# Two attentions that normalise their probabilities early and turn half-precision planes by DMA; gate factors written as rows

## The chip, the core and the metric

The kernel runs on one core of one Trainium2 chip. A core has a matrix engine (TensorE, PE in the profile; its weight loads are listed apart as PEld), a vector engine (VectorE, DVE), a scalar engine (ScalarE, ACT), GpSimd (POOL) and SyncE (SP), which mostly issues DMAs. Each engine runs its own instructions in order; semaphores tie the engines together. Matrix products read from the on-chip memory SBUF and write to PSUM. The metric is device time in microseconds (us) of one execution; times are compared by the median of several runs.

## The reference

The computation is two layers of a diffusion backbone with 512 latent tokens and 256 context tokens, model width 1024. Each layer normalises and modulates its input, makes one combined projection, and runs two attention branches side by side. Branch A is a 2-D neighbourhood attention (8 heads of 64; latent queries see a window of 8 rows by 16 columns, with a learned position bias, and all context keys). Branch B is grouped-query attention (8 query heads, 2 key heads, all latent and context keys, rotary positions). The softmax of both is the usual one:

```
s = einsum(q, k).astype(float32) * HEAD_DIM ** -0.5      (+ bias in branch A)
p = softmax(s, axis=-1).astype(v.dtype)
att = einsum(p, v)
o_a = (a_att * silu(a_z)) @ w_o_a
o_b = (b_att * silu(b_z)) @ w_o_b
merged = sigmoid(g_a) * o_a + sigmoid(g_b) * o_b
x_new = x + gate_x * (merged @ w_out)
```

The first layer also updates the context tokens, which attend to context only; the second layer leaves them. `gate_x` (and `gate_c` for the context) is one third of `silu(c) @ w_ada + b_ada`. All inputs and the output are float32.

## The kernel before, in words

Products keep float32 accuracy by splitting: a value is written as a rounded high part and a low remainder, and each product of two split operands is three matrix products (lines 429 to 431, `mm3`). Weights are loaded as raw tiles by SP, cast to a high part on ACT and subtracted on DVE or GpSimd (`load_w`, `load_w2`; tiles raw, whi, wlo).

The layer runs as: projections of branch A's keys, values and queries; NA, head by head; projections of branch B; GQ, head by head; then the output projections ("merge"). `pipeline` runs the heads: it issues the scores of head h, then the value products of head h-1, then some pieces of `fill`, independent projections (the gates and SiLU paths) that give PE work between the attention's steps. The order on each engine is made by a scheduler from this program order; buffers are rotating pools, and a tile is written again only when its readers are done.

In NA (`na_scores`, `na_values`) a head has four query tiles of 128, one of them the edge tile of the grid. For each tile PE makes 512 scores in PSUM (pss), DVE adds the bias and finds the greatest (L954, tile p), ACT takes the exponential with its sum (L957), and `softmax_tail` divides: DVE takes the reciprocal r of the sum and multiplies p by it and by one half, or, for query tiles 1 and 3 (`NA_POOL`), GpSimd does the multiplying (L763, L764). One head later, `transpose_split` turns p: PE transposes 128x128 blocks against an identity (L773, L775), ACT copies the result from PSUM as the high part (L781), DVE subtracts it for the low part (L782). There are four such groups of four transposes per head, and one more for the context queries in layer 0. The value products (L977 to L988) take both parts, with values split in va0 and va1.

In GQ (`gq_scores`, `gq_values`) a tile has 768 scores. DVE's pass L1127 finds the greatest value and shifts it by a constant (`P_LOG`), ACT takes the exponential (L1128), and `turned` makes two float16 planes of the undivided p: a cast on ACT (L798) and a subtraction on DVE, or on GpSimd for tiles 1 and 3 (L799), into a tile h. SP then issues a transposing DMA from h to ht (L800). The value products (L1144, L1145) read ht. The division comes last: `divide` turns the reciprocals by PE (L807) and multiplies them into the gate path (L808). `head_out` adds the two halves of the product and multiplies by the gate path z (L791 to L793). The context queries of layer 0 go the same way (tiles ct), with the subtraction on GpSimd.

The bias of NA is loaded by SP for each head (`load_bias`, L929 and L931) into single buffers. Issued by SP as well: the weight loads, the reloads of spilled gates (L656), and the gate factors. `ada_gate` makes the factors as a tile [128, 8 per vector] and writes them to DRAM transposed, element by element (L317); the merge stage reads them back as a row.

Of the kernel before, what the change touches and what calls it, by code (L numbers as in the profile page):

```python
# [25 lines left out]
NP_NA = (7, 8)  # L26
# [3 lines left out]
NT_NA = 2  # L30
P_LOG = 9.7
# [39 lines left out]
def hybrid_kernel(es: ExitStack, tc, x, ctx, cvec, w_ada, w_ada0, small, gvec, w_in, w_o_a, w_o_b, w_out,  # L71
# [238 lines left out]
    def ada_gate(l, nv):  # L310
# [6 lines left out]
        nc.sync.dma_start(gd[l][0:n].rearrange("n p -> p n"), g[:, 0:nv].rearrange("p v k -> p (v k)"))  # L317
# [232 lines left out]
    def split_v(ps, hi, lo, hi_src=None):  # L550
        S.copy(R(hi), ps)
        V.tensor_tensor(R(lo), ps, hi, ALU.subtract)

    def evac_va(dsts):
        def f(t, ps):
            d = dsts[t // 3].rearrange("p (t n) -> p t n", t=3)[:, t % 3, :]
            d = d.rearrange("p (r q d) -> p r q d", q=4, d=64)
            s = ps.rearrange("p (r e d) -> p r e d", e=2, d=64)
            hi, lo = d[:, :, 0:4:3, :], d[:, :, 1:3, :]
            split_v(s, hi, lo)  # L560
        return f
# [18 lines left out]
    def layer(l, hx, nxt, start):  # L580
# [8 lines left out]
        def gate_steps(halves, pool):  # L589
            return (ada_steps(l, range(16, 24), halves, nv, pool)  # L590
                    + ([lambda: ada_gate(l, nv)] if 1 in halves else []))
# [133 lines left out]
        va = [big("va0"), big("va1")]  # L725
        w = load_w(W, C_AV, 512, KT, mix_lo)
        for t in range(6):
            tok_proj(w, 512, a_hx, t, evac_va(va))
# [16 lines left out]
        for t in range(qt):  # L745
            tok_proj(w, 512, a_hx, t, evac_na(qav, True, gq, YB if first else 4))
            run(bg, per_bg)
# [7 lines left out]
        if True:  # L755
            def softmax_tail(p, n, r, pieces, eng=None):

                V.reciprocal(r, r)
                for i, (c0, c1) in enumerate(pieces):
                    if eng is None:  # L760
                        V.tensor_scalar(p[:, c0:c1], p[:, c0:c1], r[:, i:i + 1], 0.5, ALU.mult, ALU.mult)
                    else:
                        G.tensor_scalar(r[:, i:i + 1], r[:, i:i + 1], 0.5, None, ALU.mult)  # L763
                        G.tensor_tensor(p[:, c0:c1], p[:, c0:c1],  # L764
                                        r[:, i:i + 1].to_broadcast([128, c1 - c0]), ALU.mult)

            def transpose_split(blocks, n0=0, n1=512):

                att["turn"] += 1
                pt = psw(512, "s" if att["spare"] and att["turn"] % 2 else "t")  # L770
                for src, c0 in blocks:
                    if c0 is None:
                        T.transpose(pt.rearrange("p (s n) -> p s n", n=64)[:, 0:8:7, :], src, ident)  # L773
                    else:
                        T.transpose(pt[:, c0:c0 + 128], src, ident)  # L775
                if att["spare"]:
                    hi, lo = R(p_tile()[:, 0:512]), R(p_tile()[:, 0:512])
                else:
                    hi = att["p"].tile([128, 512], F32R, tag="pth", name=nm("pth"), bufs=att["nt"])
                    lo = att["p"].tile([128, 512], F32R, tag="ptl", name=nm("ptl"), bufs=att["nt"])  # L780
                S.copy(hi[:, n0:n1], pt[:, n0:n1])  # L781
                V.tensor_tensor(lo[:, n0:n1], pt[:, n0:n1], F(hi[:, n0:n1]), ALU.subtract)  # L782
                return hi, lo

            def head_out(po, e, dst, eng=None):
# [5 lines left out]
                S.copy(a, po[o:o + 64, :n])  # L791
                V.tensor_tensor(a, po[m:m + 64, :n], a, ALU.add)
                (eng or G).tensor_tensor(dst, dst, a, ALU.mult)  # L793

            def turned(p, n, out, eng):

                h = att["p"].tile([128, 2, n], F16, tag="h", name=nm("h"), bufs=att["nh"])
                S.copy(h[:, 0], p[:, :n])  # L798
                eng.tensor_tensor(h[:, 1], p[:, :n], h[:, 0], ALU.subtract)  # L799
                nc.sync.dma_start_transpose(out, h.rearrange("p a n -> p (a n)"))  # L800

            def divide(ps, r, e, dst, back):

                n = r.shape[-1]
                V.reciprocal(r, r)
                for i in range(n):
                    T.transpose(ps[:, 128 * i:128 * i + 128], r[:, i:i + 1].to_broadcast([128, 128]), ident)  # L807
                V.scalar_tensor_tensor(dst, ps[64 * e:64 * e + 64, :128 * n], back[64 * e:64 * e + 64], dst,  # L808
                                       ALU.mult, ALU.mult)

            def shrink(v, s, mx, row):

                V.tensor_reduce(mx[:, 0:1], v, AX, ALU.max)
                V.tensor_reduce(mx[:, 1:2], v, AX, ALU.min, negate=True)
                V.tensor_tensor(mx[:, 0:1], mx[:, 0:1], mx[:, 1:2], ALU.max)
                pt = psw(512, "t")
                T.transpose(pt[0:1, 0:128], mx[:, 0:1], ident)
                V.tensor_reduce(row[:, 0:1], pt[0:1, 0:128], AX, ALU.max)
                T.matmul(pt[:, 128:129], row[:, 0:1].to_broadcast([1, 128]), ident[0:1, 0:1], start=True, stop=True)
                V.tensor_scalar(s[:, 1:2], pt[:, 128:129], 1.0e-30, 1.0 / V_UP, ALU.max, ALU.mult)  # L820
                V.reciprocal(s[:, 0:1], s[:, 1:2])
                V.tensor_scalar(s[:, 1:2], s[:, 1:2], 0.5, None, ALU.mult)
# [40 lines left out]
            def ctx_scores(q, kh, kl, ct=None):  # L863
# [7 lines left out]
                if ct is not None:  # L871
                    V.tensor_scalar(mx, mx, P_LOG, None, ALU.add)
                p = p_tile()
                r = sp.tile([128, 2], F32, tag="r", name=nm("r"), bufs=8)
# [3 lines left out]
                if ct is not None:  # L878
                    turned(p, 512, ct.rearrange("p a i k n -> p (a i k) n"), G)
                    return ct, r  # L880
                softmax_tail(p, 512, r, [(0, 256), (256, 512)])
                return p

            def ctx_values(p, vsl, dst, e, back=None):
                if back is not None:
                    ct, r = p
                    ps = psw(512, "v")
                    po = ps[:, 0:256]
                    divide(ps[:, 256:512], r, e, dst, back)
                    for k in range(2):  # L890
                        for a in range(2):
                            T.matmul(po.rearrange("p (i n) -> p i n", i=2), vsl(4 + k), ct[:, a, :, k, :],
# [603 lines left out]
```

## Time and profile before

| | us |
|---|---|
| median of three runs | 1131.86 |
| lowest, highest | 1130.71, 1135.87 |
| profiled execution | 1136.54 |
| its span in the trace | 1134.8 |
| busy PE, DVE, ACT, POOL | 1092.4, 765.3, 578.0, 490.5 |

The profile is of one execution. Busy time is the union of an engine's instructions; matrix products overlap each other, so a busy PE need not be at its peak rate. A line of the groups gives source line, engine, operation, tiles, shapes and count, then busy time and the mean ns of one, then the idle time just ahead of it with what ended it. "SPq" and the like are the queues in which an engine issues DMAs. A row of the waits gives the waiting engine and line, what it waited for, then total us, number of times, and the longest.

### The profile page before, as it was taken

To read this page: it belongs to the slowest core of one execution; us is meant where nothing else is said; L and a number is where in the kernel's file an instruction comes from. 1 tells how busy PE (TensorE), PEld (TensorE's weight loads), DVE (VectorE), ACT (ScalarE), POOL (GpSimd) and SP (SyncE) were. 2 spreads that over 40 slices of the span, in tenths; PEclk is the share of its full clock that TensorE was granted. 3 is DMA by queue.
4 is the path that set the end of the run, shared out by engine and by line. 5 is a ranking of instruction groups with operands and counts; after the bars stand their busy time and mean duration, and the time that the engine had idled before them with its cause. 6 is when DMAs were issued, how large, how long until landed. Compare 5 with 4: busy or idle time off the path is not lost.

```text
span 1134.8 us, 16867 instructions
## 1 busy us (share of the span) xinstructions
PE 1092.4 (96%) x5824; PEld 905.5 (80%) x5824; DVE 765.3 (67%) x1492; ACT 578.0 (51%) x1152; POOL 490.5 (43%) x405
## 2 busy tenths in 40 slices
PE   8999999999999999779999999999999999999998
PEld 5688888888988877557788888887888987777677
DVE  4666788888365478636567895357988765677473
ACT  6463266656333566555331275325666545776431
POOL 1044255654246245345521454335554563463530
PEclk9999999999999999989999999999999999999999
DMA  9454412233341597679733542453333236989742
GB/s 366 148 173 134 126 49 66 83 125 98 110 140 47 130 205 176 108 216 248 192 104 127 158 149 77 142 182 72 108 105 112 64 103 164 186 219 250 198 147 81
DMA packets 195278, 161.29 MB, mean 142 GB/s; under 512 B 119444, under 2 KB 161144, under 8 KB 193528
## 3 DMA queue, kind: packets, MB, share of 16 engines
q1 hardware_dynamic: 187856, 145.82, 47.2%
q0 software_dynamic: 2368, 7.87, 2.1%
q10 hardware_dynamic: 4968, 6.53, 1.7%
q8 instruction: 46, 0.75, 0.3%
q14 instruction: 40, 0.33, 0.1%
HBM read 115.58 MB, written 17.32 MB: 117 GB/s over the span
## 4 chain that ended last, share of the span: by engine, by line
PE 78%; DMA 6%; DVE 5%; issue 5%; POOL 3%; ACT 2%; SPq 1%; POOLq 0%; ACTq 0%; DVEq 0%
PE psx L431 11%; PE psx L430 11%; PE psx L429 11%; PE psf L429 9%; PE psf L430 8%; PE psf L431 8%; PE pst L775 2%; PE pss L951 2%; PE pss L857 2%; PE pss L858 2%; DMA raw<-in_w_in_dram 2%; DMA ht<-h 1%; PE pst L521 1%; PE pst L1144 1%; PE pst L1145 1%
## 5 line engine op out<-in xcount | busy, mean ns | idle before, releaser
L429 PE MATMUL psf<-hx,whi 128*128 128x512 f32 (+1 forms) x360 | 137.9, 383 | 4.1 <-ACT zt L610 2.5
L416 POOL TENSOR_TENSOR wlo<-raw,whi 128x512 fp32r<-128x512 f32 x70 | 98.0, 1405 | 94.4 <-ACT whi L414 64.3
L431 PE MATMUL psf<-hx,wlo 128*128 128x512 f32 (+1 forms) x360 | 135.8, 377 | 0.0
L430 PE MATMUL psf<-hx,whi 128*128 128x512 f32 (+1 forms) x360 | 135.2, 376 | 0.0
L429 PE MATMUL psx<-whi,hx 128*128 128x512 f32 (+1 forms) x328 | 120.7, 371 | 0.0
L430 PE MATMUL psx<-wlo,hx 128*128 128x512 f32 (+1 forms) x328 | 119.7, 366 | 0.0
L431 PE MATMUL psx<-whi,hx 128*128 128x512 f32 (+1 forms) x328 | 119.5, 365 | 0.0
L414 ACT CAST whi<-raw 128x512 fp32r<-128x512 f32 x136 | 82.5, 620 | 72.6 <-DMA raw<-in_w_in_dram 44.9
L402 POOL TENSOR_TENSOR wlo<-raw,whi 128x512 fp32r<-128x512 f32 x40 | 61.0, 1528 | 120.6 <-ACT whi L399 73.0
L799 POOL TENSOR_TENSOR h<-p,h 128x768 f16<-128x768 f32 (+1 forms) x40 | 64.9, 1626 | 99.7 <-ACT h L798 79.1
L399 ACT CAST whi<-raw 128x512 fp32r<-128x512 f32 x88 | 54.4, 623 | 100.4 <-PE psx L431 33.9
L500 POOL TENSOR_TENSOR ss<-ss,ehalf 128x8 f32<-128x8 f32 (+2 forms) x40 | 62.2, 1558 | 74.1 <-DVE ss L497 74.0
L416 DVE TENSOR_TENSOR wlo<-raw,whi 128x512 fp32r<-128x512 f32 x66 | 66.6, 1009 | 28.9 <-ACT whi L414 27.4
L1127 DVE CUSTOM_DVE_ANT_0 p<-pss,vb 128x768 f32<-128x768 f32 x64 | 60.2, 953 | 36.7 <-PE pss L858 19.9
L429 PEld LDWEIGHTS psf<-hx,whi 128*128 128x128 f32 x360 | 67.9, 189 | 16.1 <-ACT zt L610 3.6
L431 PEld LDWEIGHTS psf<-hx,wlo 128*128 128x128 f32 x360 | 67.8, 188 | 11.5
L430 PEld LDWEIGHTS psf<-hx,whi 128*128 128x128 f32 x360 | 67.9, 189 | 10.3
L1128 ACT ACTIVATE p<-pss,mx 128x768 f32<-128x768 f32 x64 | 57.5, 900 | 35.0 <-DVE mx L1127 31.5
L431 PEld LDWEIGHTS psx<-whi,hx 128*128 128x128 f32 x328 | 61.9, 189 | 10.0
L430 PEld LDWEIGHTS psx<-wlo,hx 128*128 128x128 f32 x328 | 62.0, 189 | 9.2
L429 PEld LDWEIGHTS psx<-whi,hx 128*128 128x128 f32 x328 | 61.7, 189 | 8.9
L429 PE MATMUL psx<-hx,whi 128*128 128x256 f32 (+1 forms) x208 | 68.1, 327 | 0.0
(359 smaller groups left out, 3097.5 us busy)
## 6 DMA issues: line engine op xcount, KB each, us to landing
raw<-in_w_in_dram SPq DMA_DIRECT2D x168, 256.0 KB, 2.9
rawb<-in_w_ada_dram SPq DMA_DIRECT2D x48, 256.0 KB, 2.8
raw<-in_w_out_dram SPq DMA_DIRECT2D x32, 256.0 KB, 3.1
tg<-gs SPq DMA_DIRECT2D x4, 1536.0 KB, 6.4
rawx<-in_w_ada_dram SPq DMA_DIRECT2D x4, 1024.0 KB, 13.3
rawy<-in_w_ada_dram SPq DMA_DIRECT2D x4, 1024.0 KB, 10.3
gs<-zt ACTq DMA_DIRECT2D x16, 256.0 KB, 2.1
raw<-in_w_o_a_dram SPq DMA_DIRECT2D x16, 256.0 KB, 3.4
```

Of the source, the lines that this page charges most:

```text
L399: S.copy(hi[:, :n], raw[:, :n])
L402: e.tensor_tensor(lo[:, :n], raw[:, :n], F(hi[:, :n]), ALU.subtract)
L414: S.copy(hi, raw)
L416: lo_eng(i).tensor_tensor(lo, raw, F(hi), ALU.subtract)
L429: T.matmul(ps, lhs[0], rhs[0], start=first, stop=False)
L430: T.matmul(ps, lhs[0], rhs[1], start=False, stop=False)
L431: T.matmul(ps, lhs[1], rhs[0], start=False, stop=last)
L500: G.tensor_tensor(ss, ss, ehalf[:, :n], ALU.pow)
L775: T.transpose(pt[:, c0:c0 + 128], src, ident)
L799: eng.tensor_tensor(h[:, 1], p[:, :n], h[:, 0], ALU.subtract)
L1127: V.tensor_tensor_reduce(p, pss, lift, -1.0, 3e38, ALU.add, ALU.min, mx[:, 0:1])
L1128: S.activation(p, pss, AF.Exp, bias=mx[:, 0:1], accum_out=r[:, i:i + 1])
```

## The change

Both attentions now divide before they turn. `turned` replaces `softmax_tail`, `transpose_split` and `divide`. It takes the reciprocal of the row sums, scales it by 2 to the 14th (`P_UP`), and makes two float16 planes of the normalised p. On query tiles 0 and 2, ACT's cast applies the factor and DVE does multiply and subtract in one instruction; on tiles 1 and 3 GpSimd scales r, multiplies p, and subtracts, with ACT's plain cast in between. Context tiles take the first form, two halves each. SP then issues the transposing DMAs; NA's edge tile needs two of them, for 64 rows each, as its columns of the turned tile lie apart.

NA's values become float16 planes too: each of the six tiles is copied to vf and its greatest magnitude found by an absolute-value pass on ACT and a maximum on DVE (`size`); after the first query tile `split_va` makes one common factor (`shrink`, two small PE steps) and the planes (`halves`). Two of the nine large buffers change their use: vf and one f16 tile in place of va0 and va1, and then `spare` for the turned tiles of even heads and the context. `head_out` applies the factor back. The pools are smaller: p tiles 3 and 4 by layer in place of 7 and 8, h tiles 3 and 4. NA's products no longer use the PSUM pool v for latent queries.

In GQ, DVE's shift by a constant gives way to a plain maximum. The factors of `ada_gate` are turned by PE, copied by ACT and written as whole rows.

```diff
+        pt = psw(512, "t")
+        T.transpose(pt[0:n, 0:128], g[:, 0:nv].rearrange("p v k -> p (v k)"), ident)
+        gt = pool.tile([16, 128], F32, tag="agt", name=nm("agt"), bufs=1)
+        S.copy(gt[0:n], pt[0:n, 0:128])
+        nc.sync.dma_start(gd[l][0:n], gt[0:n])
-        nc.sync.dma_start(gd[l][0:n].rearrange("n p -> p n"), g[:, 0:nv].rearrange("p v k -> p (v k)"))
...
+    def size(v, junk, mx):
+        S.activation(junk, v, AF.Abs)
+        V.tensor_reduce(mx, junk, AX, ALU.max)
+    def halves(v, d, s):
+        S.activation(d[:, :, 0, :], v, AF.Copy, scale=s)
+        V.scalar_tensor_tensor(d[:, :, 1, :], v, s, d[:, :, 0, :], ALU.mult, ALU.subtract)
...
+            def turned(p, n, out, eng, r=None):
+                h = att["p"].tile([128, 2, n], F16, tag="h", name=nm("h"), bufs=att["nh"])
+                if r is not None:
+                    V.reciprocal(r, r)
+                    eng.tensor_scalar(r, r, P_UP, None, ALU.mult)
+                    w = n // r.shape[-1]
+                if r is None or eng is G:
+                    if r is not None:
+                        G.tensor_tensor(p, p, r.to_broadcast([128, n]), ALU.mult)
+                    S.copy(h[:, 0], p[:, :n])
+                    eng.tensor_tensor(h[:, 1], p[:, :n], h[:, 0], ALU.subtract)
+                else:
+                    for i in range(n // w):
+                        c = slice(w * i, w * i + w)
+                        S.activation(h[:, 0, c], p[:, c], AF.Copy, scale=r[:, i:i + 1])
+                        V.scalar_tensor_tensor(h[:, 1, c], p[:, c], r[:, i:i + 1], h[:, 0, c], ALU.mult, ALU.subtract)
+                for o, (n0, n1) in out:
+                    nc.sync.dma_start_transpose(o, h[n0:n1].rearrange("p a n -> p (a n)"))
...
             def na_scores(h, q, kh, kl):
-                    softmax_tail(p, 512, r[:, 0:1], [(0, 512)], G if i in NA_POOL else None)
+                    at = [(0, 64, 0), (448, 512, 64)] if i == 0 else [(128 * i - 64, 128 * i + 64, 0)]
+                    turned(p, 512, [(ht[:, :, a:b], (n, n + b - a)) for a, b, n in at],
+                           G if i in NA_POOL else V, r[:, 0:1])
...
             def na_values(h, ht):
+                for k in range(2):
+                    for a in range(2):
+                        T.matmul(po, vsl(4 + k), ht[:, 4 * a + 2 + k, :], start=k + a == 0, stop=False)
+                for t, part in enumerate((((0, 192, 0),), ((64, 192, 1), (192, 320, 0)),
+                                          ((192, 320, 1), (320, 448, 0)), ((320, 512, 1),))):
+                    for n0, n1, k in part:
+                        for a in range(2):
+                            T.matmul(po[:, n0:n1], vsl(t), ht[:, 4 * a + k, n0:n1], start=False,
+                                     stop=t == 3 and a == 1)
...
             def gq_scores(q, kh, kl):
-                    V.tensor_tensor_reduce(p, pss, lift, -1.0, 3e38, ALU.add, ALU.min, mx[:, 0:1])
+                    V.tensor_reduce(mx[:, 0:1], pss, AX, ALU.max, negate=True)
-                    turned(p, 768, ht[:, i], G if i in SPLIT_POOL else V)
+                    turned(p, 768, [(ht[:, i], (0, 128))], G if i in SPLIT_POOL else V, r[:, i:i + 1])
...
             def gq_values(h, ht):
-                divide(psw(512, "t"), r, e, dst, vs[:, 1:2])
```

More of the change, by code (lines that the diff above doesn't have):

```diff
@@ L755, in layer, with head_out @@
         if True:
[L756 to L785, printed above, removed]
+            def head_out(po, e, dst, back, eng=None):
                 n = dst.shape[-1]
@@ L1018, in na_first, with values_of @@
                 q = stage_q(qav[:, j, :], e)
-                ps_ = na_scores(h, q, kh, kl)
-                return ps_, ctx_scores(q, kh, kl) if first else None
-            def values_of(dst, f, back=None):
+                st = na_scores(h, q, kh, kl)
+                if not first:
+                    return st, None
+                o = 4096 + 1024 * (h % 2)
+                ct = spare[:, o:o + 1024].rearrange("p (a i k n) -> p a i k n", a=2, i=2, k=2)
+                return st, ctx_scores(q, kh, kl, ct)
+            def values_of(dst, f, back):
                 def g(h, st):
```

195 lines of the change are left out of this document (80 added, 115 removed).

## The prediction

> **What bounds the kernel now.** I read the busy times first, then the engines in stretches of time, then what ended PE's longest pauses, then the queue of SP.
>
> ```profile
> span 1134.8 us, 16867 instructions
> PE 1092.4 (96%) x5824; PEld 905.5 (80%) x5824; DVE 765.3 (67%) x1492; ACT 578.0 (51%) x1152; POOL 490.5 (43%) x405
> PE 78%; DMA 6%; DVE 5%; issue 5%; POOL 3%; ACT 2%; SPq 1%; POOLq 0%; ACTq 0%; DVEq 0%
> ```
>
> PE is busy 96% of the span and carries 78% of the chain that ended last. What takes work from PE's queue shortens the kernel where PE is full, as long as nothing else becomes late. Where it is full, the stretches tell. Their columns are the length, then busy time of PE, weight loads, DVE, ACT and POOL (with counts), the granted clock, the DMA share and GB/s.
>
> ```profile
> 150.00:305.00 155.00, 155.00 (x971) 138.38 (x970) 121.36 (x272) 93.02 (x212) 75.29 (x74) 1.00 0.28 87
> 383.00:465.00 82.00, 78.26 (x455) 63.86 (x454) 62.88 (x122) 55.63 (x109) 36.13 (x25) 1.00 0.83 173
> 465.00:485.00 20.00, 9.88 (x61) 8.70 (x59) 9.41 (x15) 8.55 (x19) 4.85 (x4) 0.86 0.64 115
> 485.00:562.00 77.00, 66.89 (x346) 51.71 (x347) 41.78 (x73) 40.78 (x78) 37.65 (x27) 0.90 0.79 206
> 770.00:895.00 125.00, 122.64 (x671) 104.74 (x670) 105.39 (x203) 81.85 (x167) 66.79 (x62) 1.00 0.33 95
> 955.00:1074.00 119.00, 113.31 (x535) 84.95 (x534) 79.91 (x126) 79.68 (x142) 63.27 (x43) 1.00 0.95 218
> ```
>
> 150 to 305 us is neighbourhood attention (NA) of layer 0, 770 to 895 that of layer 1: PE full, DVE at 78% and 84%, DMA a third used. 383 to 562 and 955 to 1074 are grouped-query attention (GQ), which already turns its probabilities by DMA: PE is idle 4.6% and 4.8% of two of these stretches, 13% of 485 to 562, and half of 465 to 485. That hole has one cause:
>
> ```profile
> 464.93 0.37 SPq L317 DMA_DIRECT2D gd<-ag  x1
> ...
> 467.89 16.43 SPq L800 DMA_TRANSPOSE ht<-h  x3
> ...
> 486.71 0.59 PE L1144 MATMUL pst<-ht,vb 128*128 128x512 f16 x1 [11.83 <-DMA ht<-h]
> ...
> 767.69 0.38 SPq L317 DMA_DIRECT2D gd<-ag  x1
> ...
> 772.23 12.04 SPq L411 DMA_DIRECT2D raw<-in_w_in_dram  x4
> ```
>
> Twice the kernel writes the gate factors element by element (L317), and both times SP's next transfers stall: three turns take 16.43 us, later four weight loads 12.04 us. The first time PE waits 11.83 us.
>
> **The change part by part.** (a) Transposes on PE. Their pace shows where they stand among other matmuls:
>
> ```profile
> 219.18 0.40 PE L429 MATMUL psf<-hx,whi 128*128 128x512 f32 x1
> 219.41 0.27 PE L773 MATMUL pst<-ident,p 128*128 128x128 f32 x1
> 219.52 0.49 PE L775 MATMUL pst<-ident,p 128*128 128x128 f32 x3
> 219.77 0.48 PE L430 MATMUL psf<-hx,whi 128*128 128x512 f32 x1
> 220.08 0.39 PE L431 MATMUL psf<-hx,wlo 128*128 128x512 f32 x1
> ...
> L775 PE MATMUL pst<-ident,p 128*128 128x128 f32 x212 | 35.3, 272 | 0.0
> L773 PE MATMUL pst<-ident,p 128*128 128x128 f32 x60 | 16.0, 272 | 0.0
> L807 PE MATMUL pst<-ident,r x64: 270/272/417, 395.6 to 1059.2; 128*128 128x128 f32 x64
> L807 PE MATMUL psv<-ident,r x16: 270/271/417, 399.6 to 549.5; 128*128 128x128 f32 x16
> ```
>
> From 219.41 to 220.08 four transposes and one 512-column matmul pass, 0.67 us. Such a matmul alone takes 0.23 us (219.18 to 219.41), so a transpose holds PE for 0.11 us; the listed 272 ns are latency. The code has 16 per head in NA and 4 for context queries in layer 0: 256 + 32 = 288, removed at 31.7 us. The late division goes too, 80 transposes of L807, 8.8 us. Together -40.5 us, nearly all of it in stretches where PE is at 95% or more.
>
> (b) Gate factors as rows. One PE transpose, one small copy, then a write of whole rows. It removes the 11.83 us; the clock missing in that stretch, 0.14 x 20 = 2.8 us, of which half lay under work (-1.4); and 1.9 us near 772 (PE's 122.64 of 125, less 0.5 for other causes): -15. Kept at nothing: the stall had another cause and stays. I take -15, because two of two such writes are followed by the same stall.
>
> (c) Value products in NA become f16. Per head, eight matmuls of 128 columns and four of 192 stand for eight of 192 or 256. Narrow ones may be held by the weight load:
>
> ```profile
> L1144 PEld LDWEIGHTS <-vb 128*128 128x128 f16 x96 | 9.5, 99 | 26.6 <-issue 14.1 <-DMA ht<-h 3.4
> L782 DVE TENSOR_TENSOR ptl<-pst,pth 128x512 fp32r<-128x512 f32 x35 | 23.5, 682 | 3.2 <-ACT pth L781 3.0
> L781 ACT CAST pth<-pst 128x512 fp32r<-128x512 f32 x35 | 19.8, 583 | 7.0 <-PE pst L775 5.1 <-PE psv L901 1.4
> L761 DVE TENSOR_SCALAR p<-p,r 128x512 f32<-128x512 f32 x32 | 23.8, 744 | 0.7
> L764 POOL TENSOR_TENSOR p<-p,r 128x512 f32<-128x512 f32 x32 | 35.1, 1096 | 2.6
> L763 POOL TENSOR_SCALAR r<-r 128x1 f32<-128x1 f32 x32 | 10.8, 339 | 61.7 <-DVE r L758 40.7 <-ACT za L610 5.3 <-ACT p L957 3.6
> L799 POOL TENSOR_TENSOR h<-p,h 128x768 f16<-128x768 f32 x32 | 55.3, 1727 | 83.3 <-ACT h L798 67.5 <-issue 10.0 <-PE psf L431 5.1
> L799 POOL TENSOR_TENSOR h<-p,h 128x512 f16<-128x512 f32 x8 | 9.8, 1219 | 16.3 <-ACT h L798 11.6 <-issue 4.7
> L798 ACT CAST h<-p 128x512 f16<-128x512 f32 x8 | 4.9, 618 | 9.1 <-DMA ht<-h 9.0
> ```
>
> At worst 4 x 0.1 us more for each of 16 heads, 6 us; at best a little less than before. I take +2, and +1 for the scaling of the values (two small PE steps that wait on DVE, per layer).
>
> (d) Engines beside PE in NA. DVE loses the low halves (72 at 0.68 us or a little less) and the normalising passes (32 x 0.74, 16 half ones), and gets 32 fused ones, priced like L782's 0.68, and 8 pairs of half ones; it drops by some 40 us over both layers. ACT swaps 0.58 us casts for 0.62 us ones. POOL gets 16 subtractions of 1.22 us a layer, 75 to 95 us of 140, and 67 to 86 of 112. All lie beside PE; uncovered, POOL's would be 20 us a layer. The new value staging (12 absolute-value passes and six scaled halves, about 14 us on ACT by the cast's price) lies in projections where PE is full: nothing, or 14 us if ACT blocked PE's tiles.
>
> (e) SP. Each NA head issues five turns (the edge tile in two pieces), six in layer 0: 48 and 40 new ones.
>
> ```profile
> L800 SPq DMA_TRANSPOSE ht<-h x64: 1273/1594/12456, 388.6 to 1060.1; - x64
> ht<-h SPq DMA_TRANSPOSE x64, 4.3
> L800 SPq DMA_TRANSPOSE ct<-h x4: 1232/1426/2273, 418.4 to 551.0; - x4
> 1017.03 24.77 SPq L800 DMA_TRANSPOSE ht<-h  x10
> L929 SPq DMA_DIRECT2D bint<-in_bias_int_dram x16: 332/341/532, 133.9 to 871.2; - x16
> L411 SPq DMA_DIRECT2D raw<-in_w_in_dram x104: 367/378/818, 81.4 to 969.9; - x104
> L931 SPq DMA_DIRECT2D bedg<-in_bias_edge_dram x32: 465/562/803, 135.5 to 865.8; - x32
> SPq L800 <- POOL h L799: 26.3, 10, 5.7
> ```
>
> The rows give least, median and greatest ns of an issue. Unloaded, 48 x 1.43 = 69 us; queued back to back, ten GQ turns took 2.48 us each, and at two thirds of the size 1.65, so 79 us. The bias loads (0.34 + 2 x 0.56 per head) and about 24 weight loads of 0.38 add 21. That is 90 to 100 us of about 140 in layer 0, 78 to 91 of 112 in layer 1: it fits, with little room. But SP serves in order: a turn that waits for GpSimd holds the next head's bias and the weights behind it, and who waits for these is DVE's score pass and ACT's casts. The other way back is the h tile: with three (layer 0) or four of them all in turns, ACT's next cast waits, and the exponentials behind it. DMA bandwidth fits: GQ's share of 0.95 against NA's 0.33 gives (0.95-0.33) x 119 / 32 = 2.3 us per turn, 1.5 for NA's size, so about 0.75 of both NA stretches.
>
> The new wait on these turns is not in the trace of before. Bounds: nothing, and GQ's worst stretch, 13% of 240 us = 31. I take GQ's usual 4.7%, since it is the same chain with fewer bytes: +11.
>
> By the Trainium skill, "TensorE: Matmul & The Clock Gate", Part 1, an idle window of about 3.4 us halves PE's clock. The trace agrees (granted clock 0.86 in the stretch with the 11.83 us pause). By that rule the same 11 us, if they came as three or four lumps, would cost an estimated 5 us more.
>
> (f) GQ's longer chain. Two of four tiles now get a GpSimd scale (0.34) and multiply (1.10 x 1.5 = 1.64) before the cast: 2.0 us later each, and POOL 63 to 95 of 119 in layer 1. Bounds: nothing, or all 16 of a layer exposed, 32 us. DVE's score pass stops writing the p tile, so p is held about as long as before; I take +4.
>
> Sum: -40.5 - 15 + 2 + 1 + 11 + 4 = -37.5. The profiled execution took 1136.5 us around its span, 4.7 above the median of 1131.86; carried over to the median, 1131.9 - 37.5 = 1094.4, say 1095.
>
> **The rivals.** Full gain: turns always land in time, (e) and (f) are zero: 1131.9 - 52.5 = 1079. For it: a head later is where the values are needed, some 15 us against a landing of 4.3. Against: GQ never got below 4.6% idle.
>
> Swallowed: PE's relief in NA is lost to waits for turns (e) at 31 us and (f) at 8: -40.5 - 15 + 3 + 39 = -13.5, 1118. For it: 485 to 562. Against: part of that stretch is the hole's aftermath.
>
> Slower: SP's order becomes the bound in NA. With a mean slot s per turn (issue plus waiting at the queue's head), both NA stages last 88 s + 42 us, against 280 now. (b), GQ's 8.8 of (a), (c) and (f) make -17 elsewhere, so the kernel is slower from s = (280 + 17 - 42) / 88 = 2.9 us. At 3.3 the stages last 332, and it is 1131.9 + 52 - 17 = 1167. For it: ten of 72 turns waited a mean 2.6 us for GpSimd, which here gets a pass more per tile. Against: with 1.43 to 1.65 us of issue it takes 1.25 us or more of waiting on every single turn, and the ten make 0.4.
>
> The stall is not the element write: -37.5 + 15, 1110; it stays inside the swallowed case's range.
>
> **How the numbers follow.** As forecast 0.45 (its own range 1086 to 1106), full gain 0.22, swallowed or the stall kept 0.19, slower 0.14. The range 1075 to 1122 takes in the first three and leaves out the slow case and the edges. A measurement here tells 0.5% (6 us) from no change: slower 0.13, same 0.04 (the tail of the swallowed case), faster 0.83.
>
> **What would show it.** Right: no 128x128 transposes of p or r; PE busy near 1050 us; no pause above 5 us after the gate write, and its neighbours on SP at their median; both NA stretches 10 to 17 us shorter; PE idle about 5% in them, ended by the DMA of ht. Wrong: SP's turns waiting longer than 2 us on POOL in the mean, DVE's score pass waiting for the bias DMA, or POOL above 85% in layer 1's GQ with PE waiting for a wlo made on POOL.

## The result

The changed kernel took 1163.04 us (median of four runs, 1161.60 to 1164.15), the kernel before 1132.19 beside it: a ratio of 1.0266, 95% interval 1.0249 to 1.0283. It is 31 us slower where 37.5 us faster was forecast. The profiled execution, 1161.60 us, has a span of 1159.8 against 1134.8. First its span and busy times:

```profile
span 1159.8 us, 16671 instructions
PE 1075.3 (93%) x5528; PEld 868.4 (75%) x5528; DVE 799.8 (69%) x1478; ACT 611.4 (53%) x1188; POOL 592.3 (51%) x493
```

PE's idle time, span less busy, went from 42.4 to 84.5 us. Its busy time fell by 17.1 us only, since the mean granted clock fell from 0.989 to 0.974: the clock is either full or half in the records, so that is 2 x 0.026 x 1159.8 = 60 us at half clock against 25 before, and by an estimate (half clock counted as half the work) the difference cost some 17 us. By this estimate about 35 us of work left PE, as forecast; 17 came back as slow clock and 42 as idle time, and that is the 25 us between the spans. By stages, from a stage's first score to its last value product (NA and GQ of layer 0, NA and GQ of layer 1; columns as in the prediction), after:

```profile
153.30:300.70 147.40, 131.90 (x766) 108.39 (x765) 122.67 (x251) 98.58 (x213) 93.03 (x87) 0.95 0.71 155
388.60:565.80 177.20, 147.94 (x794) 118.11 (x793) 129.74 (x213) 109.24 (x210) 101.78 (x78) 0.94 0.77 177
800.90:905.80 104.90, 93.81 (x490) 73.19 (x489) 80.63 (x163) 72.64 (x145) 78.75 (x70) 0.95 0.79 175
959.60:1096.80 137.20, 124.25 (x539) 90.93 (x537) 93.50 (x129) 87.43 (x150) 101.10 (x77) 0.95 0.85 189
```

and the same stages before:

```profile
152.50:305.40 152.90, 152.90 (x957) 136.46 (x956) 118.89 (x270) 92.79 (x210) 73.59 (x72) 1.00 0.29 89
383.50:558.00 174.50, 150.52 (x835) 120.49 (x835) 111.57 (x205) 103.68 (x201) 75.43 (x54) 0.94 0.79 180
783.20:890.90 107.70, 106.60 (x582) 91.31 (x582) 92.13 (x185) 72.68 (x151) 56.74 (x56) 1.00 0.35 105
948.20:1070.30 122.10, 116.41 (x550) 87.61 (x550) 80.64 (x128) 82.85 (x148) 65.89 (x44) 1.00 0.92 208
```

In layer 0 NA looks a little shorter, but only because projections that ran beside it now stand outside it: from its first NA score to its first GQ score it is 383.5 - 152.5 = 231.0 us before and 388.6 - 153.3 = 235.3 after. In layer 1 the same stretch did get shorter, from 948.2 - 783.2 = 165.0 to 959.6 - 800.9 = 158.7 us. PE, which had hardly a gap in NA, is now idle a tenth of it. GQ of layer 1 is 15 us longer. In all four stages POOL has more to do. The groups, one line per shape (busy us, mean ns, idle time ahead and what ended it; line numbers shift a little from kernel to kernel):

```profile
L828 DVE SCALAR_TENSOR_TENSOR h<-p,r,h 128x768 f16<-128x768 f32 x32 | 48.8, 1524 | 12.1 <-ACT h L827 11.8
L828 DVE SCALAR_TENSOR_TENSOR h<-p,r,h 128x512 f16<-128x512 f32 x32 | 40.0, 1249 | 8.4 <-ACT h L827 8.1
L823 POOL TENSOR_TENSOR h<-p,h 128x768 f16<-128x768 f32 x32 | 55.7, 1742 | 17.7 <-ACT h L822 16.5 <-PE pss L866 0.9 <-POOL zb L792 0.2
L821 POOL TENSOR_TENSOR p<-p,r 128x768 f32<-128x768 f32 x32 | 51.6, 1611 | 2.3
```

DVE's fused pass, priced at 0.68 us for 512 columns, takes 1.25. A GQ tile holds POOL for 1.61 + 1.74 us. What PE waited for, and one wait each of DVE and ACT (total us, times, longest):

```profile
PE pss L865 <- ACT p L1111: 11.4, 5, 6.9
PE psf L433 <- ACT zt L621: 11.3, 9, 4.6
PE psv L891 <- DMA ht<-h: 8.1, 3, 4.6
PE psf L433 <- DVE tg L699: 7.5, 7, 2.0
PE pst L1125 <- DMA ht<-h: 4.9, 2, 2.8
PE pst L967 <- DMA ht<-h: 4.7, 5, 1.3
DVE p L948 <- DMA bint<-in_bias_int_dram: 5.6, 4, 2.7
ACT h L822 <- POOL p L821: 37.5, 30, 3.2
```

PE now waits for exponentials, for emptied projection banks (zt, tg) and for turns alike: everything that ACT and DVE serve is late by turns. The longest pause, 6.93 us, shows one cause: the passes of line 420 on DVE (least, median, greatest ns), and the timeline there (start, duration):

```profile
L420 DVE TENSOR_TENSOR wlo<-raw,whi x66: 665/693/8844, 97.7 to 1078.7; 128x512 fp32r<-128x512 f32 x66
```

```profile
500.81 7.12 POOL L664 TENSOR_TENSOR gal<-za,gah 128x768 fp32r<-128x768 f32 x4
501.30 8.84 DVE L420 TENSOR_TENSOR wlo<-raw,whi 128x512 fp32r<-128x512 f32 x1 [0.68 <-ACT whi L418]
507.90 1.63 POOL L823 TENSOR_TENSOR h<-p,h 128x768 f16<-128x768 f32 x1
...
515.46 0.79 PE L865 MATMUL pss<-gk,qs 128*128 128x512 f32 x1 [6.93 <-ACT p L1111]
```

POOL works off five passes without a gap. A DVE subtraction with both operands in SBUF, 0.69 us at its median, begins under the first of them and ends at 510.14, only after the fifth has ended at 509.53. Behind it stand other passes and the next tile's score maximum, then the exponential, then PE.

### The profile page after: what moved, and what is told of

Same layout as the page of the kernel before. It is cut to its first block, busy times and chain, and to the rows that moved or that the text cites. A ratio compares the mean times of both kernels' runs of the same rounds, so it can differ in the third digit from the quotient of the medians.

```text
span 1159.8 us, 16671 instructions
## 1 busy us (share of the span) xinstructions
PE 1075.3 (93%) x5528; PEld 868.4 (75%) x5528; DVE 799.8 (69%) x1478; ACT 611.4 (53%) x1188; POOL 592.3 (51%) x493
## 5 line engine op out<-in xcount | busy, mean ns | idle before, releaser
L420 POOL TENSOR_TENSOR wlo<-raw,whi 128x512 fp32r<-128x512 f32 x70 | 106.4, 1525 | 78.8 <-ACT whi L418 55.9
L828 DVE SCALAR_TENSOR_TENSOR h<-p,r,h 128x512 f16<-128x512 f32 (+2 forms) x96 | 119.2, 1252 | 26.0 <-ACT h L827 25.3
L406 POOL TENSOR_TENSOR wlo<-raw,whi 128x512 fp32r<-128x512 f32 x40 | 59.4, 1489 | 141.2 <-ACT whi L403 79.9
L823 POOL TENSOR_TENSOR h<-p,h 128x512 f16<-128x512 f32 (+1 forms) x64 | 98.2, 1535 | 26.1 <-ACT h L822 24.5
L420 DVE TENSOR_TENSOR wlo<-raw,whi 128x512 fp32r<-128x512 f32 x66 | 72.9, 1105 | 39.8 <-ACT whi L418 39.3
L821 POOL TENSOR_TENSOR p<-p,r 128x512 f32<-128x512 f32 (+1 forms) x64 | 86.3, 1349 | 4.3
L827 ACT ACTIVATE h<-p,r 128x512 f16<-128x512 f32 (+2 forms) x96 | 67.3, 717 | 19.2 <-issue 7.2
L433 PEld LDWEIGHTS psx<-whi,hx 128*128 128x128 f32 x328 | 61.9, 190 | 10.8 <-DVE mx L948 1.9
```

Source lines behind the costliest of these rows:

```text
L406: e.tensor_tensor(lo[:, :n], raw[:, :n], F(hi[:, :n]), ALU.subtract)
L420: lo_eng(i).tensor_tensor(lo, raw, F(hi), ALU.subtract)
L433: T.matmul(ps, lhs[0], rhs[0], start=first, stop=False)
L821: G.tensor_tensor(p, p, r.to_broadcast([128, n]), ALU.mult)
L827: S.activation(h[:, 0, c], p[:, c], AF.Copy, scale=r[:, i:i + 1])
L828: V.scalar_tensor_tensor(h[:, 1, c], p[:, c], r[:, i:i + 1], h[:, 0, c], ALU.mult, ALU.subtract)
```

## The experiments

Ratios are to the kernel before, measured beside each run; 1% is 11.3 us.

### The parts one by one

Rows alone. Edit: only `ada_gate` in the kernel before.

```diff
-        nc.sync.dma_start(gd[l][0:n].rearrange("n p -> p n"), g[:, 0:nv].rearrange("p v k -> p (v k)"))
+        T.transpose(pt[0:n, 0:128], g[:, 0:nv].rearrange("p v k -> p (v k)"), ident)
+        S.copy(gt[0:n], pt[0:n, 0:128])
+        nc.sync.dma_start(gd[l][0:n], gt[0:n])
```

> The kernel before with one edit: the gates' factors are turned on TensorE and stored as rows; both attentions stay as they were. Theory A (the rows remove the 11.8 us wait of TensorE for a turn at 485 to 558 us and the loss lay elsewhere): 1116 to 1124 us against 1132 before, and no wait of over 5 us for ht<-h at that place. Rival (another work of the gates, not the element write, held the turns up, or the freed time is waited elsewhere): 1128 to 1136 us.

Measured 1127.24 us, ratio 0.9952 (0.9937 to 0.9967): 5 us gained, less than theory A allowed and more than its rival. Its waits and its timeline at the place:

```profile
PE psv L811 <- DVE ho L796: 6.9, 1, 6.9
PE pst L1148 <- DMA ht<-h: 3.0, 3, 1.6
```

```profile
491.53 7.14 POOL L657 TENSOR_TENSOR gal<-za,gah 128x768 fp32r<-128x768 f32 x4
492.19 8.25 DVE L420 TENSOR_TENSOR wlo<-raw,whi 128x512 fp32r<-128x512 f32 x1
```

The 11.8 us wait for the turn is gone, so the element write was its cause. In its place comes a wait of 6.9 us for DVE, which stood behind POOL's row of four, and one pass more, for 8.25 us.

NA changed, GQ as before. Edit: in the changed kernel GQ's and its context's tiles go undivided to `turned`, and `divide` is back.

```diff
-                    turned(p, 768, [(ht[:, i], (0, 128))], G if i in SPLIT_POOL else V, r[:, i:i + 1])
+                    turned(p, 768, [(ht[:, i], (0, 128))], G if i in SPLIT_POOL else V)
...
+                divide(psw(512, "t"), r, e, dst, vs[:, 1:2])
```

> The changed kernel with grouped-query attention put back (late division, undivided turn); rows and neighbourhood attention stay changed. Theory A (early normalising in both attentions is what costs, the neighbourhood half giving its removed transposes back as waits, the grouped-query half adding chain): 1138 to 1148 us, so 15 to 25 us under the changed kernel's 1163, and 15 to 25 us above the run with rows alone. Theory B (the loss is all in grouped-query attention, neighbourhood attention gains as its 288 fewer transposes say): under 1110 us. Theory C (the loss is all in neighbourhood attention): 1158 us or more.

GQ changed, NA as before: the reverse, on top of rows.

> The kernel before with rows and with grouped-query attention normalised early, two of four tiles on GpSimd; neighbourhood attention as it was. Theory A: 1133 to 1145 us, 15 to 25 us above the run with rows alone. Theory B: about 1163 us or more, as all of the loss and none of the gain is in it. Theory C: within 5 us of the run with rows alone. If the two halves do not act on each other, this run's distance to rows alone and that of the run with late division in grouped-query attention add up to the changed kernel's.

Measured 1140.00 (1.0053, 1.0034 to 1.0072) and 1157.29 (1.0215, 1.0186 to 1.0244). Against rows, the NA half costs 1.0% and the GQ half 2.6%, 11 and 30 us; their sum is a little more than the 3.1% between rows and the changed kernel. Both halves lose; GQ's is the greater, and above what theory A gave it.

Both undivided to the end. Edit: NA too passes its tiles undivided, with the constant in the exponential's bias, and `divide` after the value products.

> The changed kernel with both attentions undivided until the end: neighbourhood tiles too are turned by DMA as they leave the exponential (raised by a constant in its bias), and one multiply per head with the turned factors divides them, at the price of four transposes per head. Theory N (normalising early, its multiplies on GpSimd and its longer chain to the turn, makes TensorE wait): 1100 to 1118 us, TensorE's waits for ht<-h in neighbourhood attention under 3 us in layer 0 against 10.9 us in the changed kernel. Theory T (turning by DMA as such is too late for neighbourhood attention): within 6 us of the run that has only grouped-query attention put back, the waits for ht<-h as long as in the changed kernel.

Measured 1131.21 (0.9979, 0.9966 to 0.9992). Late division takes 0.7% off the NA half, 9 us, where theory N gave 22 to 40 and theory T at most 6. TensorE still waits 6.2 us for ht in NA.

### Who pays for dividing early

Order on ACT. Edit: on GpSimd's tiles ACT applies the factor in its cast, ahead of GpSimd's multiply; the factor is scaled on DVE.

```diff
-                    eng.tensor_scalar(r, r, P_UP, None, ALU.mult)
+                    V.tensor_scalar(r, r, P_UP, None, ALU.mult)
...
-                        G.tensor_tensor(p, p, r.to_broadcast([128, n]), ALU.mult)
-                    S.copy(h[:, 0], p[:, :n])
+                        S.activation(h[:, 0], p[:, :n], AF.Copy, scale=r)
+                        G.tensor_tensor(p, p, r.to_broadcast([128, n]), ALU.mult)
```

> The changed kernel; on the tiles that GpSimd normalises, ScalarE writes the upper plane itself as a scaled copy straight after the exponential (the scale made on VectorE), and GpSimd's multiply follows it, so that ScalarE's queue no longer stands behind GpSimd. The same passes, in another order. Theory Q (ScalarE, in order, waits 37.5 us for GpSimd's product at the cast of the upper plane, and the next exponentials and the fills' tanh, for which TensorE waits, stand behind it): the wait falls under 5 us and the time to 1135 to 1150 us against 1163. Theory P (VectorE's fused pass, 1.25 us on average where it takes 0.75 undisturbed, is what delays the planes): 1158 us or more. Theory L (the chain to the turn is too long for the place of the value products): 1155 us or more.

Measured 1161.35 (1.0260, 1.0233 to 1.0287): no gain. ACT no longer waits for POOL's product; it waits instead at the exponential, among others for

```profile
ACT p L1113 <- DVE h L830: 25.0, 7, 9.1
```

so ACT's place behind GpSimd was not the limit, and theory Q falls.

No tile on GpSimd.

```diff
-NA_POOL = (1, 3)
-SPLIT_POOL = (1, 3)
+NA_POOL = ()
+SPLIT_POOL = ()
```

> The changed kernel with no tile on GpSimd: all four tiles of a head take ScalarE's scaled copy and VectorE's fused pass. Theory Q: 1135 to 1152 us, as ScalarE no longer waits for GpSimd, less what 64 more fused passes of 1.25 us and more on VectorE cost where it then stands. Theory P: the fused pass's mean falls by 0.2 us and more, since GpSimd runs beside it more seldom, and the time to 1145 to 1155 us. If VectorE is what is short: 1165 to 1185 us.

Measured 1130.02 (0.9980, 0.9961 to 0.9999): 33 us under the changed kernel, better than any theory gave. All of the loss against before goes with GpSimd's tiles, though DVE took 64 more passes (of the 5 us that rows alone gain, it keeps 2).

The same in the GQ half alone (`SPLIT_POOL = ()` in that half's kernel).

> The kernel before with rows and with grouped-query attention normalised early as in the run of that half alone (1157 us), but with all four of its tiles on ScalarE and VectorE. Theory S (the loss is GpSimd's two passes per tile, 3.2 us against 1.1 us, and what they slow on VectorE; normalising early is by itself nearly free): 1124 to 1136 us, 20 us and more under that half with GpSimd. Rival E (normalising early costs by itself, whoever does it): 1145 us or more.

Measured 1131.80 (0.9987, 0.9974 to 1.0000) against 1157.29. GQ of layer 1 in the kernels with rows alone, with the GQ half on two engines, and with that half off GpSimd:

```profile
939.80:1061.20 121.40, 116.52 (x551) 87.58 (x550) 81.20 (x128) 82.88 (x148) 65.83 (x44) 1.00 0.92 209
```

```profile
954.00:1098.20 144.20, 127.26 (x538) 93.13 (x536) 96.72 (x129) 87.90 (x150) 97.89 (x77) 0.93 0.82 181
```

```profile
937.00:1061.30 124.30, 117.38 (x534) 89.66 (x534) 97.07 (x164) 89.80 (x153) 43.16 (x28) 0.99 0.93 213
```

144.2 us with POOL busy for 97.89, 124.3 with 43.16. DVE, with 35 instructions more, is busy for no longer than with POOL beside it (97.07 against 96.72). Dividing early by itself costs 0.35% over rows.

The exponential of DVE's tiles kept in PSUM.

```diff
-                    p = p_tile()
+                    p = p_tile() if i in NA_POOL else pss
...
+                    if i not in SPLIT_POOL:
+                        p = pss
```

> The changed kernel; on VectorE's two tiles of each head the exponential stays in the scores' bank of PSUM, so that VectorE's fused pass has one operand in SBUF in place of two. Theory P: its mean falls from 1249 and 1524 ns to 0.75 to 0.85 and 1.0 to 1.1 us, and the time to 1140 to 1150 us, unless the scores' banks, held 3 us longer, make TensorE wait, which its waits at the score products would show. If the two SBUF operands do not matter, the mean stays above 1.2 us.

Measured 1148.12 (1.0130, 1.0090 to 1.0169). The fused passes:

```profile
L828 DVE SCALAR_TENSOR_TENSOR h<-pss,r,h 128x768 f16<-128x768 f32 x32 | 32.5, 1015 | 14.8 <-ACT h L827 14.2 <-issue 0.6
L828 DVE SCALAR_TENSOR_TENSOR h<-pss,r,h 128x512 f16<-128x512 f32 x32 | 23.9, 746 | 6.6 <-ACT h L827 6.3
```

1015 and 746 ns in place of 1524 and 1249, with POOL almost as busy (570 us against 592): about 0.5 us of each pass was time held up with two SBUF operands, 32 us of DVE in all (48.8 + 40.0 against 32.5 + 23.9). It is GpSimd beside the pass that does it, and not the operand's place by itself: in the trace of the kernel with no tile on GpSimd, 41 of the 64 passes of 512 columns, both operands in SBUF, had no GpSimd instruction beside them and took 0.73 to 0.75 us, while the other 23 took a mean of 1.23. Here 30 of the 32 had one beside them, and none took more than 0.752. The time falls by 15 us. How much of that is the operand alone is not shown: these tiles also stop using p buffers, and score products now wait for the banks (PE for L828, 12.0 us).

By the Trainium skill, "SBUF — State Buffer", section "Who interferes with whom", a VectorE instruction with two SBUF inputs contends with a GpSimd instruction that reads SBUF. The trace agrees (the 0.5 us above). Of VectorE's two-port modes the section says that whoever issues first gets the shared pair for the whole instruction. What the trace shows goes beyond one instruction: at 501 us DVE waited for a row of five.

One GpSimd pass a tile. Edit: the multiply on GpSimd's tiles left out.

```diff
-                        G.tensor_tensor(p, p, r.to_broadcast([128, n]), ALU.mult)
```

> The changed kernel without GpSimd's multiply on its tiles, so that a tile there has one pass of GpSimd, the subtraction, in place of two; these tiles' weights are left undivided, so the output is not the attention's. If the second pass is what turns GpSimd's tiles into the loss: 1128 to 1138 us against 1163 with it and 1130 with no tile on GpSimd. If any tile on GpSimd costs that, or VectorE's contention with the subtraction does: 1148 us or more.

Measured 1148.65 (1.0157, 1.0129 to 1.0185), just on the rival's side. Its timeline shows what came in between:

```profile
498.58 7.12 POOL L664 TENSOR_TENSOR gal<-za,gah 128x768 fp32r<-128x768 f32 x4
498.69 9.87 DVE L817 TENSOR_SCALAR r<-r 128x2 f32<-128x2 f32 x1
...
1006.24 11.06 DVE L826 SCALAR_TENSOR_TENSOR h<-p,r,h 128x768 f16<-128x768 f32 x1
1007.43 1.66 POOL L821 TENSOR_TENSOR h<-p,h 128x768 f16<-128x768 f32 x1
1009.05 1.28 POOL L420 TENSOR_TENSOR wlo<-raw,whi 128x512 fp32r<-128x512 f32 x1
1010.31 4.96 POOL L664 TENSOR_TENSOR gal<-za,gah 128x512 fp32r<-128x512 f32 x4
1015.23 1.25 POOL L420 TENSOR_TENSOR wlo<-raw,whi 128x512 fp32r<-128x512 f32 x1
```

Twice DVE stood for about 10 us behind a row of POOL passes; even a pass over two columns did. Leaving out the second pass is thus worth 14 of the 33 us. The other 19 stay, and the run does not say how much of them is such rows (the changed kernel has one stall of this kind, the kernel with no tile on GpSimd one of 7.11 us).

That row of four on VectorE.

```diff
-            hilo(za, gated["a"], range(4))
+            hilo(za, gated["a"], range(4), V)
```

> The changed kernel, with the lower halves of the gated neighbourhood output (line 664, four subtractions issued in a row, 7.1 us of GpSimd in layer 0 and 5 us in layer 1) made on VectorE. Theory H (while GpSimd works pass behind pass, a VectorE pass with its operands in SBUF does not come through: one weight subtraction of 0.69 us stood for 8.84 us at 501 us, over those four passes and the one behind them): no VectorE pass over 5 us is left, TensorE's waits for the exponential near 508 us (6.9 us) go, and the time is 1148 to 1157 us against 1163. Rival (the long pass is a hole in the records, and the wait has another cause): 1160 us or more.

Measured 1157.28 (1.0217, 1.0180 to 1.0254). The trace has no DVE pass over 4.6 us, and PE's waits between 480 and 530 us have come down to these and shorter ones on tg:

```profile
PE psf L433 <- ACT zt L621: 4.6, 1, 4.6
PE pss L865 <- ACT p L1111: 1.2, 1, 1.2
```

So the 6.9 us pause went with the row, as theory H says. Its 6 us are at the limit of the measurement, the two intervals just overlapping.

The bare kernel off GpSimd: `NA_POOL = ()` and `SPLIT_POOL = ()` on rows; and the same on the kernel with both attentions undivided.

> The kernel before with rows, its neighbourhood tiles all normalised and its grouped-query tiles all split on VectorE, none on GpSimd. If GpSimd's tiles cost there too, though each has one pass in place of two: 1116 to 1123 us against 1127 for rows alone. If GpSimd with one pass a tile was free or a relief for VectorE: 1127 to 1140 us, and then it is the second pass that turned it into a loss.

> The run in which both attentions are undivided until the end (1131 us), with no query tile on GpSimd: one subtraction on VectorE each, only the context's planes still on GpSimd. Theory S: 1112 to 1124 us. If one pass a tile on GpSimd costs nothing: 1129 to 1136 us.

Measured 1124.91 (0.9936, 0.9918 to 0.9955) and 1130.78 (0.9976, 0.9963 to 0.9989), so 0.2% under rows and nothing under the other: with one pass a tile and an undivided p, GpSimd's tiles were neither loss nor relief. `hilo` on VectorE, on top of rows off GpSimd:

> The kernel before with rows and no query tile on GpSimd (1125 us), with those four subtractions on VectorE. Theory H: 1115 to 1121 us if one of its VectorE passes stood behind GpSimd there too, as one of 8.25 us did in the run of rows alone; else 1122 to 1128 us.

1130.98 (0.9976, 0.9959 to 0.9993), 6 us worse, outside both guesses: in that kernel's trace no DVE pass stood behind the row (none over 2.7 us), and DVE got the work for nothing.

### Where the freed time of TensorE went

More time for the turns.

```diff
-                    if prev is not None:
-                        values_of(h - 1, prev)
                     run(fill, len(fill) - (n - n * min(h + 1, spread) // spread))
+                    if prev is not None:
+                        values_of(h - 1, prev)
```

> The changed kernel with the order of one head altered: the fill's projections are issued ahead of the value products of the head before, not after them, so that the turned planes have some 8 us more. Theory L: TensorE's waits for ht<-h fall from some 19 us to under 5 us and the time to 1140 to 1150 us. Theory Q: the waits for the turns go, those for the exponential and the tanh (over 22 us) stay; 1152 to 1160 us.

Measured 1157.90 (1.0215, 1.0185 to 1.0244), in theory Q's band, 5 us under the changed kernel. The waits for turns fell from 17.7 to some 10 us, not under 5; the others stayed. A longer way to the turn is a small part.

The removed transposes as dead work, in the kernel with no tile on GpSimd.

```diff
+                for n in range(18):
+                    T.transpose(po[:, 128 * (n % 4):128 * (n % 4) + 128], ident, ident)
```

> The changed kernel with no tile on GpSimd (1130 us), and 18 transposes of a constant put ahead of the value products of each neighbourhood head, into a bank that the products then overwrite: 288 in all, TensorE's removed work as dead work. If TensorE's freed time lies in waits (for the turned planes, for VectorE, which was 91% busy in the first layer's stage) and in the half clock that follows them: 1126 to 1140 us, TensorE's idle time about 20 us less and its time at half clock about 15 us less. If the removal of the transposes is a gain that something else hides: 1160 us or more, their 31 us on top.

Measured 1141.23 (1.0077, 1.0047 to 1.0106) against 1130.02, both with no tile on GpSimd; it is 1 us above the guess for waits and slow clock. Busy times without, in a span of 1130.5 us, then with them, in 1139.8:

```profile
PE 1066.6 (94%) x5528; PEld 868.0 (77%) x5528; DVE 815.3 (72%) x1606; ACT 614.4 (54%) x1188; POOL 386.4 (34%) x301
```

```profile
PE 1089.4 (96%) x5816; PEld 892.0 (78%) x5816; DVE 806.8 (71%) x1606; ACT 616.2 (54%) x1188; POOL 395.0 (35%) x301
```

288 transposes at the prediction's 0.11 us are 31.7 us of work; they cost 11 us. PE's idle time fell from 63.9 to 50.4 us, and with the mean clock at 0.990 in place of 0.979 the time at half clock fell from 2 x 0.021 x 1130.5 = 47 to 23 us, worth 12. So taking transposes out of NA was worth about a third of their time in this kernel. What limits there is not PE alone: in layer 0's NA of the kernel without dead work DVE is busy 118.37 of 130 us:

```profile
152.90:282.90 130.00, 122.08 (x740) 103.70 (x738) 118.37 (x282) 97.68 (x211) 45.33 (x37) 0.97 0.76 166
```

The exponential in PSUM for all NA tiles, none on GpSimd, relieves that DVE.

> The changed kernel with no tile on GpSimd (1130 us), and with the neighbourhood tiles' exponential left in the scores' bank of PSUM, so that their fused pass has one operand in SBUF. If the pass's port matters beside what GpSimd still does (the weights' lower planes): its mean at 512 columns falls from 920 to about 750 ns and the time to 1120 to 1127 us. If it does not, or the banks held longer make the score products wait: 1129 to 1137 us, with waits of the score products for VectorE's fused pass.

Measured 1125.53 (0.9937, 0.9920 to 0.9955), 5 us less, with the pass at

```profile
L828 DVE SCALAR_TENSOR_TENSOR h<-pss,r,h 128x512 f16<-128x512 f32 x64 | 46.8, 747 | 10.1 <-ACT h L827 8.9 <-DMA raw<-in_w_in_dram 0.7 <-DMA bedg<-in_bias_edge_dram 0.2
```

in place of 920 ns.

### What beats both kernels

NA from PSUM on ACT and DVE alone, turned by DMA; GQ undivided as before; rows.

> What the runs point to: rows; neighbourhood tiles turned by DMA, normalised on ScalarE and VectorE alone from the scores' bank of PSUM; grouped-query attention undivided as before, with one pass of GpSimd on two of four tiles. From 1125.5 us (all on VectorE, the exponential in PSUM) less the 4 to 7 us by which the late division was ahead in grouped-query attention (1132 early, on VectorE, against 1125 to 1127 for rows): 1117 to 1123 us. If the freed time is again waited for elsewhere: 1123 to 1130 us.

1123.09 (0.9920, 0.9897 to 0.9943), on the border of the two guesses: ahead of both its parts, but within their intervals. With `hilo` on VectorE, whose row held up a DVE pass for 8.2 us in that run's trace:

> The combination that ran at 1123 us, with those four subtractions on VectorE. Theory H: 1113 to 1120 us, no VectorE pass over 5 us. Rival: 1121 us or more.

1120.16 (0.9878, 0.9847 to 0.9908), 14 us under the kernel before and 43 under the changed one; span 1115.0, mean clock 0.991. Its longest DVE pass is 3.5 us. It is the fastest kernel here, though its margin over the one before it is within the intervals, and its 1120.16 lies between theory H and the rival. Against rows with no query tile on GpSimd (0.9936), which leaves both attentions as they were, it gains 0.6%.

## Why the prediction was wrong

The steps that failed are (f), "+4", and the sentence of (d) that GpSimd's and VectorE's passes "all lie beside PE". Their work does, but not their delays.

- (f) GQ's longer chain, +4 within 0 to 32. Measured 24 us (the changed kernel against the one with GQ put back) to 30 us (over rows), with (a)'s removed divisions in it. The two added microseconds on a tile were right (means of 0.36 and 1.61 measured); I let an eighth of one layer's 32 us show, and the bound itself leaves out the other layer, whose 16 tiles make it 64. Off GpSimd, the whole GQ half costs 4 us over rows. The rest is GpSimd's tiles.
- (d) In NA DVE was to fall by some 40 us (the rows given add up to some 50). In NA's two stages it fell by 7.7 (211.0 to 203.3); in GQ's it rose by 31.0 (192.2 to 223.2), and over the whole kernel by 34.5. The fused pass was priced by a subtraction whose one operand lay in PSUM (0.68 us). Kept in PSUM, it does take 0.75; with both in SBUF beside a busy POOL it took 1.25. A nearer row stood among the groups of before, DVE's own subtraction of h, both operands in SBUF, with a mean of 1186 ns for 768 columns:

```profile
L799 DVE TENSOR_TENSOR h<-p,h 128x768 f16<-128x768 f32 x32 | 38.0, 1186 | 20.0 <-ACT h L798 19.8
```

It was not used as the price. I took POOL's 20 us a layer as harmless so long as they fit; POOL at 74% in layer 1's GQ (101.10 of 137.2) never came to the 85% I named as a sign.
- (a) -40.5 of PE work was right as work (about 35, with (c) in it), wrong as time. "Nearly all of it in stretches where PE is at 95% or more" does not give time when DVE, busy 118.89 of 152.90 us there, comes next: in the kernel with no tile on GpSimd a third of it counted.
- (b) -15. The wait of 11.83 us did vanish; the gain was 5. What would be late next was not asked. In that run it was a wait of 6.9 us behind the row of four on GpSimd; but with no query tile on GpSimd, where no DVE pass stood so long, only 2 us more were gained, so what kept the rest of the 15 is open.
- (e) SP fitted, as forecast:

```profile
L830 SPq DMA_TRANSPOSE ht<-h x152: 1194/1296/6799, 158.7 to 1085.6; - x152
ht<-h SPq DMA_TRANSPOSE x152, 3.7
SPq L830 <- DVE h L828: 56.6, 30, 6.5
SPq L830 <- POOL h L823: 39.5, 20, 4.8
SPq L830 <- DVE r L816: 19.4, 10, 4.3
```

Issue and landing are a little under the price (1.30 us against 1.43 to 1.65, and 3.7 against 4.3), and SP's waits ahead of the turns are (56.6 + 39.5 + 19.4) / 160 = 0.7 us a turn, far from the slow rival's 2.9 - 1.3. (Two figures there are off: layer 1's 91 us should be 40 x 1.65 + 21 = 87, and the rival starts from 280 us where (e) counts 140 + 112; from 252 it would begin at 2.6 us a turn.) TensorE's waits for turns in NA, 8.1 + 4.7 = 12.8 us, were near the +11. The slowdown I allowed for had the right sign and the wrong cause; that 1163 lies near its 1167 is chance. Of the three signs I named for it one came up, small: DVE's score pass waited 5.6 us for the bias, four times. SP waited for POOL 20 times, a mean of 1.98 us, and POOL in GQ stayed under 85%. Of the signs for being right, PE's busy time came to 1075 us, not near 1050, and its idle time in NA to a tenth, not 5%.
- The clock: +5 was a side estimate; by the estimate above it cost some 17 us. The rule of the Trainium skill, "TensorE: Matmul & The Clock Gate", Part 1, asks for an idle window of about 3.4 us. The last rows of this text show half clock after a shorter pause.

Not split further: of the 33 us of GpSimd's tiles, how much is DVE's fused passes held up (the PSUM run gained 15 us, with more than that changed), how much its other passes held up by GpSimd's, and how much the 3.35 us for which POOL holds a tile's p and h buffers. The row of four, worth 6 us in the run that took it away, is hardly part of it: it stands in the kernel with no tile on GpSimd too, and holds a DVE pass there for 7.11 us. The value products in f16, (c), were not measured alone.

## What to carry to other kernels

A pass given to an engine that is "half idle" is not free when that engine shares something with the next one in line: price VectorE passes by a row with the same operand places and the same neighbour, and look at where GpSimd's passes stand in an unbroken row. When PE is full and the next engine is at 80%, count removed PE work at a fraction until a run with dead work in its place has said how much (a third, here). And where a known stall is removed, look on the same timeline for what would have stalled under it.

## What the runs showed of the hardware

Two things I had not expected. A VectorE pass can wait through several GpSimd passes, not only the one running: 8.84, 8.25, 9.87 and 11.06 us in the rows above, for passes that take 0.2 to 1.0 us with no GpSimd instruction beside them. And the clock can halve after shorter pauses than I reckoned with. In the changed kernel PE paused twice for less than 2 us, at 185.7 us for 1.94 and at 194.3 for 1.85, and was busy without a gap between:

```profile
182.00:188.00 6.00, 4.06 (x30) 2.82 (x29) 5.86 (x13) 4.70 (x11) 3.87 (x5) 1.00 0.75 175
188.00:194.00 6.00, 6.00 (x42) 5.44 (x39) 5.91 (x8) 4.84 (x11) 4.20 (x5) 1.00 0.86 146
194.00:200.00 6.00, 4.15 (x14) 3.09 (x13) 5.84 (x12) 2.95 (x7) 5.61 (x6) 0.78 0.48 114
200.00:206.00 6.00, 6.00 (x39) 4.79 (x38) 3.73 (x12) 5.15 (x11) 2.44 (x4) 0.93 0.76 147
```

After the first pause the granted clock stays at 1.00. After the second it is 0.78 in that stretch and 0.93 in the next, which is (0.22 + 0.07) x 6 = 1.7 us of lost clock on top of the 1.85 us: this pause cost nearly twice its length. Why one of two pauses of almost the same length halved the clock and the other did not, the rows do not show.
